# Two feed-forward layers' first 1024 inner columns taken token tile by token tile, with ScalarE-only evacuations and casts, later conditioning and packed planner priorities

## The chip, the cores and the metric

One NeuronCore of a Trainium2 chip runs the whole program. The metric is device time in microseconds of one execution. The core has five engines that run side by side: TensorE (PE; its weight loads are listed as PEld), VectorE (DVE), ScalarE (ACT), GpSimd (POOL) and SyncE (SP, here only the queue that issues weight loads).

## The reference, cut to what matters

Two blocks of two layers each work on 256 tokens by 1024 features, in float32. Layer i of the first block is

```python
mod = silu(c) @ ada_w[i] + ada_b[i]               # c: one vector of 1024
sh1, sc1, g1, sh2, sc2, g2 = split(mod, 6)        # "conditioning": six vectors of 1024
h = rms_norm(x, norm_mix[i]) * (1 + sc1) + sh1
x = x + g1 * mixer(h)                             # i=0 chunked attention, i=1 gated MLP (gmlp)
h = rms_norm(x, norm_ffn[i]) * (1 + sc2) + sh2
x = x + g2 * (square(relu(h @ ffn_w1[i])) @ ffn_w2[i])   # 1024 -> 4096 -> 1024
```

The second block runs two attention layers (`block2`), each a normalisation, eight projections, two kinds of attention, an output projection and a normalisation of its result.

## The kernel before, in words

**Tiles.** The 256 tokens are two tiles of 128, t=0 and t=1. All weights come from HBM as one stream of items of 128 by 1024 floats (`ITEMS`), two items to a DMA, into a ring of four such pairs. For a product close to float32 precision an item is split: `item` casts it to a rounded high half (L881 on ACT, L882 on DVE), and DVE subtracts that from the original for the low half (L885). A product then is three matmuls, L782 to L784 (`mm3`). Split items lie in one arena `R` with the transposed activations `hT` and the hidden activations: at most `NHL = 9` of them, and one is placed only if `SPARE = 5120` of the arena's 25 x 1024 + 256 floats per partition stay free beside it. Each takes 2048.

**Feed-forward (`ffn`).** `norm_T` transposes the normalised rows of a token tile (L810), applies the conditioning (L1015, L1021: shift number 3, scale number 4) and splits the result (L988, L990). Inner columns come in blocks of 128. Most blocks are made by `ws_block`: eight 256-wide products with the weight as the stationary side, both token tiles at once. The first 512 columns are made by rows (`xs_group`): for one token tile at a time, eight 512-wide products, an evacuation (`copy`), four transposes, then relu and square (`relu2`). The second matrix follows `LAGF` blocks behind, accumulating in four banks, and `out_proj` finishes token tile 0 ahead of tile 1 for the last `tail` blocks. `gate_finish` multiplies by the gate, adds to x (L721), and normalises (`norm_scale`: L931 or L933, L731, L695, L968 or L970).

**Conditioning.** A 1024 by 1024 piece of `ada_w` is eight items. They come as columns (`adc`: one DVE reduction per item, L748, result ready for one block of 128 features) or as rows (`adg`, for the pairs in `BY_ROWS`: DVE accumulates over the eight items, L740, then `fin_gate` sums over partitions with PE products L770 and evacuates).

**Order.** Nothing is issued in program order. Every operation is recorded with its engines, an estimated duration and the buffers it touches; `Sched.round` places operations one by one, and the order that results is written into each engine's queue. Operations with two entries in `alts` are placed on either engine. `schedule` makes four rounds; from each it works out when an operation is due (PE's at its start, the rest counted back from their users) and uses that as the next round's priority; the best round is kept. At run time each engine works through its queue in order and waits on semaphores.

## Time and profile before

| what | value |
|---|---|
| median of three runs (lowest, highest) | 1009.37 us (1007.86, 1009.71) |
| the profiled execution's own time | 1009.61 us |
| its span, first to last instruction | 1007.8 us |
| PE busy, DVE busy, ACT busy | 97%, 77%, 56% of the span |
| mean granted TensorE clock | 0.992 |
| weights and inputs read from HBM | 214.48 MB |
| mean rate of all DMAs | 215 GB/s |

The stages lie in the trace like this, in us from the span's start: the first projections to about 62, attention to about 117, its output projection to about 147, feed-forward 0 to about 345, gmlp to about 558, feed-forward 1 to about 735, the two attention layers of the second block to 1002, and the last normalisation. Matmuls are pipelined, so that a row of a busy PE shows more than the time to the next matmul; the spacing of starts tells the cost of one. A stage's own waits tell more than the shares of the whole span.

### The profile page before, as it was taken

The numbers are of one execution on the slowest core, as the hardware profiler recorded it, in microseconds if no ns is written. First come the engines' busy times: TensorE is split into PE (matmuls) and PEld (weight loads), VectorE is DVE, ScalarE is ACT, GpSimd is POOL, SyncE is SP. The second block draws the span as 40 slices with busy tenths as digits, with TensorE's granted clock in tenths as the row PEclk, the third lists the DMA queues.
The fourth block names the chain that finished last, engine by engine and source line by source line (L and its number), as shares of the span: only waits on it lengthen the run. The fifth ranks groups of instructions, "written<-read, shape, count | busy, mean of one in ns | idle before, by whom it ended". The sixth has DMA issues, their size and how long they took to land.

```text
span 1007.8 us, 14849 instructions
## 1 busy us (share of the span) xinstructions
PE 976.2 (97%) x5716; PEld 851.7 (85%) x5716; DVE 776.7 (77%) x1308; ACT 568.0 (56%) x1052; POOL 24.7 (2%) x60
## 2 busy tenths in 40 slices
PE   6999988999999999999999999999999999899997
PEld 5768776899999888899999899999989888799886
DVE  6899989988877986977767855645697786877982
ACT  6578736544445655644455744445455676655781
POOL 1000000010000000000000000030000000000000
PEclk9999998999999999999999999999999999899999
DMA  8987585898775595766463555565545333443401
GB/s 321 359 316 263 210 334 183 359 364 324 290 281 203 207 383 204 292 228 232 170 242 133 177 197 172 207 193 203 179 161 188 113 121 119 160 168 128 166 1 42
DMA packets 32121, 216.50 MB, mean 215 GB/s; under 512 B 3825, under 2 KB 4081, under 8 KB 7217
## 3 DMA queue, kind: packets, MB, share of 16 engines
q1 hardware_dynamic: 30816, 211.98, 56.9%
q0 software_dynamic: 1232, 3.56, 1.4%
q8 instruction: 45, 0.74, 0.3%
q14 instruction: 28, 0.22, 0.1%
HBM read 214.48 MB, written 1.05 MB: 214 GB/s over the span
## 4 chain that ended last, share of the span: by engine, by line
PE 79%; DVE 9%; ACT 5%; DMA 4%; issue 2%; SPq 0%; DVEq 0%; ACTq 0%
PE banks L782 24%; PE banks L783 24%; PE banks L784 24%; PE banks L770 4%; DMA raw<-in_wall 4%; DVE arena_r L885 3%; PE banks L810 3%; DVE arena L721 2%; ACT arena_r L881 1%; ACT arena L695 1%; DVE arena L740 1%; DVE arena L748 1%; DVE arena_r L990 1%; DMA arena<-in_xin 1%; ACT arena L710 1%
## 5 line engine op out<-in xcount | busy, mean ns | idle before, releaser
L782 PE MATMUL banks<-arena_r 128*128 128x256 f32 (+1 forms) x1632 | 563.9, 346 | 7.7 <-ACT arena_r L988 5.2
L783 PE MATMUL banks<-arena_r 128*128 128x256 f32 (+1 forms) x1632 | 554.0, 339 | 1.5 <-DVE arena_r L885 1.4
L784 PE MATMUL banks<-arena_r 128*128 128x256 f32 (+1 forms) x1632 | 553.4, 339 | 1.6 <-DVE arena_r L990 1.6
L885 DVE TENSOR_TENSOR arena_r<-raw,arena_r 128x1024 fp32r<-128x1024 f32 x300 | 359.7, 1221 | 41.8 <-ACT arena_r L881 40.4
L782 PEld LDWEIGHTS banks<-arena_r 128*128 128x128 f32 x1632 | 310.9, 191 | 43.3 <-ACT arena_r L988 8.9
L784 PEld LDWEIGHTS banks<-arena_r 128*128 128x128 f32 x1632 | 310.5, 190 | 38.3 <-DVE arena_r L990 4.7
L783 PEld LDWEIGHTS banks<-arena_r 128*128 128x128 f32 x1632 | 311.2, 191 | 35.3 <-DVE arena_r L885 4.6
L881 ACT CAST arena_r<-raw 128x1024 fp32r<-128x1024 f32 x265 | 270.5, 1044 | 85.9 <-DMA raw<-in_wall 43.4
L695 ACT ACTIVATE arena<-banks 128x256 f32<-128x256 f32 (+1 forms) x104 | 45.0, 434 | 147.2 <-PE banks L784 145.1
L988 ACT ACTIVATE arena_r<-arena 128x256 fp32r<-128x256 f32 (+1 forms) x120 | 55.8, 475 | 78.5 <-DVE arena L740 49.6
L740 DVE SCALAR_TENSOR_TENSOR arena<-banks,arena 128x256 f32<-128x256 f32 (+1 forms) x84 | 38.1, 453 | 60.7 <-ACT arena L695 42.8
L748 DVE CUSTOM_DVE_ANT_0 arena<-raw,arena 128x1024 f32<-128x1024 f32 x56 | 71.7, 1281 | 14.5 <-DMA raw<-in_wall 13.1
L695 ACT ACTIVATE arena<-arena 128x256 f32<-128x256 f32 (+8 forms) x159 | 65.1, 416 | 23.9 <-DVE arena L740 9.1
L990 DVE SCALAR_TENSOR_TENSOR arena_r<-arena,arena_r 128x256 fp32r<-128x256 f32 (+1 forms) x120 | 58.3, 494 | 24.6 <-ACT arena_r L988 23.1
L770 PE MATMUL banks<-arena 128*128 128x64 f32 (+4 forms) x448 | 70.3, 292 | 4.5 <-DMA arena<-in_ident 3.6
L770 PEld LDWEIGHTS banks<-arena 128*128 128x128 f32 x448 | 60.6, 196 | 10.1 <-ACT arena L695 3.6
L810 PE MATMUL banks<-arena 128*128 128x128 f32 x356 | 55.7, 281 | 10.1 <-DVE arena L731 4.3
L710 ACT COPY arena<-banks 128x512 f32<-128x512 f32 (+4 forms) x100 | 47.7, 488 | 31.2 <-PE banks L784 13.7
L810 PEld LDWEIGHTS banks<-arena 128*128 128x128 f32 x356 | 44.0, 147 | 21.5 <-DVE arena L731 4.6
L721 DVE TENSOR_TENSOR arena<-arena 128x512 f32<-128x512 f32 (+6 forms) x128 | 51.4, 433 | 7.6 <-ACT arena L695 3.2
L740 DVE SCALAR_TENSOR_TENSOR arena<-raw,arena 128x1024 f32<-128x1024 f32 x40 | 51.3, 1282 | 3.8 <-DMA raw<-in_wall 3.6
L721 DVE TENSOR_TENSOR arena<-banks,arena 128x512 f32<-128x512 f32 (+1 forms) x48 | 30.0, 641 | 15.3 <-PE banks L784 6.8
(45 smaller groups left out, 330.5 us busy)
## 6 DMA issues: line engine op xcount, KB each, us to landing
raw<-in_wall SPq DMA_DIRECT2D x194, 1024.0 KB, 4.9
raw<-in_wall SPq DMA_DIRECT2D x8, 512.0 KB, 9.1
arena<-in_nbias SPq DMA_DIRECT2D x4, 512.0 KB, 6.5
arena<-in_rows POOLq DMA_DIRECT2D x3, 512.0 KB, 6.0
arena<-in_xin SPq DMA_DIRECT2D x2, 512.0 KB, 5.9
out_dram<-arena SPq DMA_DIRECT2D x4, 256.0 KB, 2.4
arena<-in_dbias POOLq DMA_DIRECT2D x2, 384.0 KB, 3.6
arena<-in_wsT POOLq DMA_DIRECT2D x1, 512.0 KB, 5.9
```

Source lines behind the costliest of these rows:

```text
L695: nc.scalar.activation(out=res(out), in_=res(in_), func=func, scale=res(scale), **kw, **({"accum_out": res(accum)} if accum is not None el ...
L721: alt = ("DVE", 0.068 + n / 960.0, lambda: nc.vector.tensor_tensor(out=res(out), in0=res(a), in1=res(b), op=op))
L740: return self.S.op(("DVE", dur, lambda: nc.vector.scalar_tensor_tensor(out=res(out), in0=res(a), scalar=res(s), in1=res(b), op0=op0, op1=o ...
L748: return self.S.op(("DVE", dur, lambda: nc.vector.tensor_tensor_reduce(out=res(junk if out is None else out), in0=res(a), in1=res(b), scal ...
L770: o = self.S.op(("PE", max(n, 96) * 0.00167, lambda: nc.tensor.matmul(res(out), lhsT=res(l), rhs=res(r), start=start, stop=stop)), rd, [ou ...
L782: nc.tensor.matmul(o, lhsT=lh, rhs=rh, start=start, stop=False)
L783: nc.tensor.matmul(o, lhsT=lh, rhs=rl, start=False, stop=False)
L784: nc.tensor.matmul(o, lhsT=ll, rhs=rh, start=False, stop=stop)
L810: nc.tensor.transpose(res(o), res(i), res(ident))
L881: alts = [("ACT", 0.093 + D / 1200.0, lambda: nc.scalar.copy(out=res(hi), in_=res(src))), ("DVE", 0.068 + D / 1920.0, lambda: nc.vector.te ...
L885: dve = ("DVE", 0.068 + D / 960.0, lambda: nc.vector.tensor_tensor(out=res(lo), in0=res(src), in1=res(hi.f32()), op=ALU.subtract))
L990: self.S.op(("DVE", 0.068 + n / 960.0, lambda: nc.vector.scalar_tensor_tensor(out=res(lo), in0=res(src), scalar=scale, in1=res(hi.f32()), ...
```

## The change

The first 1024 columns of each feed-forward's inner width, not the first 512, are made by rows (`XG = 2`): tile 0's two groups, then tile 1's. The second matrix now follows eight blocks behind the first. High halves of weights are cast by ACT alone, and six kinds of evacuations and scalings of the attention that DVE could take stay on ACT. The shift of feed-forward 0 (layer 0, number 3) is now taken by columns. The conditioning of layer 1 moves back in the stream: gate 2 from the first feed-forward into gmlp's first part, gate 5 from gmlp into feed-forward 1. The second token tile's input is loaded with the first one's, ahead of all weights. The planner's due times are counted with PE's gaps taken out, and the best round's priorities are placed once more to give the order.

```diff
-BY_ROWS = ((0, 2), (0, 5), (1, 2), (1, 5), (0, 3))
+BY_ROWS = ((0, 2), (0, 5), (1, 2), (1, 5))
-LAGF = 5
+LAGF = 8
+XG = 2
-    s += pair_stream(NFF, ("w1", 0), ("w2", 0), LAGF, ada_items(0, (5,)) + ada_items(1, (0, 1, 2)))
-    e = ada_items(1, (3, 4, 5))
+    s += pair_stream(NFF, ("w1", 0), ("w2", 0), LAGF, ada_items(0, (5,)) + ada_items(1, (0, 1)))
+    e = ada_items(1, (2, 3, 4))
-    s += pair_stream(NFF, ("w1", 1), ("w2", 1), LAGF)
+    s += pair_stream(NFF, ("w1", 1), ("w2", 1), LAGF, ada_items(1, (5,)))
...
             if best is None or self.clock < best[0]:
-                best = self.clock, [(o, alt, tab, [b.off for b in o.bufs]) for o, alt, tab in out], \
-                    {b: b.off for b in self.fixed}, [(o, o.eng, o.start, o.fin) for o in self.ops]
-            due = {}
+                best = self.clock, [o.pri for o in self.ops]
+
+            due, packed, gaps, last = {}, {}, 0.0, 0.0
+            for o in sorted((o for o in self.ops if o.eng == "PE"), key=lambda o: o.start):
+                gaps += max(o.start - last, 0.0)
+                packed[o], last = o.start - gaps, o.fin
             for o in sorted(self.ops, key=lambda o: o.start, reverse=True):
-                t = o.start if o.eng == "PE" else self.clock
+                t = packed[o] if o.eng == "PE" else last - gaps
...
-            self.prev_split = S.op(alts[:1] if i < POS["w1", 0, 0] else alts, [src], [hi], after=after, pri=pri,
+            self.prev_split = S.op(alts[:1], [src], [hi], after=after, pri=pri,
...
-        self.hooks[1] = [lambda pri: load(self.x[1].v(), io["xin"][:, 1, :], 1.46, pri)]
+        load(self.x[1].v(), io["xin"][:, 1, :], 1.46, -2000)
...
-            self.act(nb[i].v(), nb[i].v(), D, scale=-1.0, dve=True)
+            self.act(nb[i].v(), nb[i].v(), D, scale=-1.0)
-                self.act(qT.v(), ps.v()[:, 0:256], 256, scale=gqk.v(), psum=True, dve=True)
+                self.act(qT.v(), ps.v()[:, 0:256], 256, scale=gqk.v(), psum=True)
...
                 for t in range(2):
-                    row = self.F(512)
-                    self.copy(row.v(), self.xs_group(t, hT, [("w1", l, q) for q in range(4)], 512, 2, (4, 5)).v(), 512,
-                              psum=True)
...
+                    for g in range(XG):
+                        row = self.F(512)
+                        self.copy(row.v(), self.xs_group(t, hT, [("w1", l, 4 * g + q) for q in range(4)], 512, 2, (4, 5)).v(),
+                                  512, psum=True)
...
-            elif f >= 4:
+            elif f >= 4 * XG:
```

The attention's copies get `both=False` in the same way; the items of the first eight `w1` blocks are cut as rows of 512 columns. Lines after the planner's part move down by 18 or 19 (L885 becomes L903).

How the order moves is shown at one boundary, the end of attention's output projection and the start of feed-forward 0. First DVE's queue of the kernel before, from where token tile 0's rows are gated and added to x (L721), squared and summed (L933), scaled by the norm (L968), a low half (L885), the conditioning of the transposed rows (L1015):

```order
L721 TENSOR_TENSOR arena<-banks,arena 128x512 x2
L721 TENSOR_TENSOR arena<-arena 128x512 x2
L933 ISA arena<-arena 128x512
L933 ISA arena 128x1
L731 TENSOR_SCALAR arena<-arena 128x1
L721 TENSOR_TENSOR arena<-banks,arena 128x512 x2
L968 TENSOR_SCALAR arena<-arena 128x512
L885 TENSOR_TENSOR arena_r<-raw,arena_r 128x1024
L1015 TENSOR_SCALAR arena<-banks,arena 128x128 x4
L882 CAST arena_r<-raw 128x1024
```

The same place in the changed kernel, from the second half of tile 0's rows on:

```order
L739 TENSOR_TENSOR arena<-banks,arena 128x512
L739 TENSOR_TENSOR arena<-arena 128x512
L951 ISA arena<-arena 128x512
L951 ISA arena 128x1
L749 TENSOR_SCALAR arena<-arena 128x1
L903 TENSOR_TENSOR arena_r<-raw,arena_r 128x1024
L986 TENSOR_SCALAR arena<-arena 128x512
L903 TENSOR_TENSOR arena_r<-raw,arena_r 128x1024
L1033 TENSOR_SCALAR arena<-banks,arena 128x128 x4
L1008 SCALAR_TENSOR_TENSOR arena_r<-arena,arena_r 128x4x128 x2
```

Before, both halves of tile 0 come together and the gating of tile 1 (the second L721 row that reads banks) stands inside tile 0's chain; now the halves come one after the other, tile 1's gating stands behind tile 0's low halves (L1008), and the cast of DVE is gone.

PE's queue at the same place, before, from the last product of the output projection: the products of `fin_gate` for the shift, tile 0's transposes, the first product of feed-forward 0.

```order
L784 MATMUL banks<-arena_r 128x512
L770 MATMUL banks<-arena 128x1 x8
L810 MATMUL banks<-arena 128x128 x8
L782 MATMUL banks<-arena_r 128x512
L783 MATMUL banks<-arena_r 128x512
L784 MATMUL banks<-arena_r 128x512
```

And in the changed kernel, around tile 0's transposes:

```order
L802 MATMUL banks<-arena_r 128x512
L828 MATMUL banks<-arena 128x128 x8
L800 MATMUL banks<-arena_r 128x512
L801 MATMUL banks<-arena_r 128x512
L802 MATMUL banks<-arena_r 128x512
```

The eight one-column products are gone. In the whole queue, the products of both tiles' output projection alternated before and ended together, and four products lay between tile 0's and tile 1's transposes; now tile 0's last product is followed by twelve of tile 1 (six ahead of tile 0's transposes, six behind), and twelve products (36 rows) lie between the two tiles' transposes.

## Rows read from the trace of the kernel before

**Rows 1.** The page's first part: busy us of each engine (share of the span), instructions.
```profile
PE 976.2 (97%) x5716; PEld 851.7 (85%) x5716; DVE 776.7 (77%) x1308; ACT 568.0 (56%) x1052; POOL 24.7 (2%) x60
```

**Rows 2.** Busy time by stretch: length, then PE, PEld, DVE, ACT, POOL, PE clock, DMA share, GB/s.
```profile
62.00:117.00 55.00, 53.15 (x289) 41.66 (x287) 53.52 (x141) 46.59 (x126) 2.07 (x4) 1.00 0.65 234
117.00:145.50 28.50, 27.14 (x138) 21.51 (x138) 25.50 (x37) 12.49 (x23) 1.44 (x2) 1.00 0.82 310
145.50:153.40 7.90, 4.94 (x34) 4.27 (x32) 7.70 (x16) 5.00 (x14) 0.00 (x0) 0.92 0.58 233
153.40:170.90 17.50, 15.40 (x61) 11.52 (x62) 16.91 (x22) 11.78 (x25) 0.00 (x0) 0.84 0.45 150
...
190.00:411.00 221.00, 221.00 (x1276) 195.04 (x1275) 183.37 (x268) 117.07 (x186) 3.54 (x6) 1.00 0.74 279
...
573.00:734.00 161.00, 161.00 (x1027) 146.69 (x1027) 94.54 (x132) 73.20 (x112) 10.28 (x28) 1.00 0.57 194
...
749.00:868.00 119.00, 118.79 (x723) 104.81 (x723) 91.40 (x198) 77.74 (x166) 2.65 (x5) 1.00 0.43 150
868.00:879.00 11.00, 7.66 (x27) 5.69 (x26) 10.81 (x18) 8.94 (x21) 0.00 (x0) 0.70 0.19 68
```

**Rows 3.** Waits of PE over the span: in total, times, longest, in us.
```profile
PE banks L810 <- DVE arena L968: 1.6, 1, 1.6
...
PE banks L782 <- ACT arena L695: 1.3, 1, 1.3
PE banks L810 <- ACT arena L710: 1.3, 2, 0.9
```

**Rows 4.** Timeline of PE at the start of feed-forward 0: start, length, what, idle before.
```profile
150.63 1.09 PE L810 MATMUL banks<-arena 128*128 128x128 f32 x8 [1.28 <-ACT arena L970]
153.55 0.79 PE L782 MATMUL banks<-arena_r 128*128 128x512 f32 x1 [1.82 <-ACT arena_r L988]
...
157.33 0.80 PE L783 MATMUL banks<-arena_r 128*128 128x512 f32 x1 [0.43 <-DVE arena_r L885]
...
158.77 0.51 PE L783 MATMUL banks<-arena_r 128*128 128x512 f32 x1
```

**Rows 5.** Timeline of DVE in the same place.
```profile
145.67 1.37 DVE L721 TENSOR_TENSOR arena<-banks,arena 128x512 f32<-128x512 f32 x2 [0.38 <-PE banks L784]
...
150.16 0.48 DVE L968 TENSOR_SCALAR arena<-arena 128x512 f32<-128x512 f32 x1
```

**Rows 6.** Groups of DVE in 62 to 146 us: count, busy us, mean ns, idle before.
```profile
L748 DVE DVE_READ_ACCUMULATOR2_ANT arena<- 128x1 f32 x40 | 3.3, 83 | 0.0
...
L713 DVE COPY arena<-banks 128x512 f32<-128x512 f32 x2 | 1.4, 690 | 0.0
...
L701 DVE TENSOR_SCALAR arena<-banks,arena 128x256 f32<-128x256 f32 x3 | 1.3, 476 | 0.0
```

**Rows 7.** Groups over the span, shapes kept apart: the three kinds of weight splitting.
```profile
L885 DVE TENSOR_TENSOR arena_r<-raw,arena_r 128x1024 fp32r<-128x1024 f32 x300 | 359.7, 1221 | 41.8 <-ACT arena_r L881 40.4
...
L881 ACT CAST arena_r<-raw 128x1024 fp32r<-128x1024 f32 x265 | 270.5, 1044 | 85.9 <-DMA raw<-in_wall 43.4 <-PE banks L784 32.3 <-PE banks L783 6.4
...
L882 DVE CAST arena_r<-raw 128x1024 fp32r<-128x1024 f32 x35 | 23.9, 686 | 2.3 <-PE banks L784 2.1 <-DMA raw<-in_wall 0.2
```

**Rows 8.** Timeline of PE, 512-wide matmuls near the end: first and last of ten.
```profile
998.73 0.39 PE L784 MATMUL banks<-arena_r 128*128 128x512 f32 x1
...
1000.77 0.39 PE L784 MATMUL banks<-arena_r 128*128 128x512 f32 x1
```

**Rows 9.** Timeline of PE, 256-wide matmuls in gmlp: first and last of eighteen.
```profile
416.72 0.28 PE L782 MATMUL banks<-arena_r 128*128 128x256 f32 x1
...
418.76 0.28 PE L784 MATMUL banks<-arena_r 128*128 128x256 f32 x1
```

**Rows 10.** The chain that ended last, merged: one batch of eight transposes, and the input's load.
```profile
3.07 7.11 DMA arena<-in_xin
...
338.21 0.88 PE banks L810 x8
```

More of the change, by code (lines that the diff above doesn't have):

```diff
@@ L116, in item_array @@
         return a["a_w_out"][0][it[1] * P:(it[1] + 1) * P]
-    if n == "w1" and it[2] < 4:
-        w = a["ffn_w1"][it[1]][it[2] * 256:(it[2] + 1) * 256, 0:512]
+    if n == "w1" and it[2] < 4 * XG:
+        g, q = divmod(it[2], 4)
+        w = a["ffn_w1"][it[1]][q * 256:(q + 1) * 256, g * 512:(g + 1) * 512]
         return w.reshape(2, P, 512).transpose(1, 0, 2).reshape(P, D)
@@ L338 @@
     EXTRA = {"DVE": 0.6}
+    SHIFTS = ()
     def __init__(self):
@@ L423, in schedule, with shift @@
                 o.pri = due[o] - (self.RUSH if o.crit else 0.0)
-        self.clock = best[0]
-        for o, o.eng, o.start, o.fin in best[3]:
-            pass
-        for b in self.fixed:
-            b.off = best[2][b]
-        return best[1]
+        pri = list(best[1])
+        for seed in self.SHIFTS:
+            self.shift(best[1], pri, seed)
+        for o, o.pri in zip(self.ops, pri):
+            pass
+        out = self.round(spaces, slots)
+        return [(o, alt, tab, [b.off for b in o.bufs]) for o, alt, tab in out]
+    @staticmethod
+    def shift(base, pri, seed):
+        rng = np.random.default_rng(seed)
+        lo, hi = min(base), max(base)
+        mid, width = rng.uniform(lo, hi), rng.choice([8.0, 20.0, 60.0])
+        size, share = rng.choice([0.7, 2.0, 5.0]), rng.choice([0.1, 0.4, 1.0])
+        for i, b in enumerate(base):
+            if abs(b - mid) < width and rng.random() < share:
+                pri[i] += size * rng.standard_normal()
     def round(self, spaces, slots):
@@ L1191, in attention @@
             for t in range(2):
-                self.copy(qkv[j][n][t].v(), acc[t, j + 3 * n].v(), 512, psum=True)
+                self.copy(qkv[j][n][t].v(), acc[t, j + 3 * n].v(), 512, psum=True, both=False)
         def second(j):
@@ L1201, in second @@
             for t in range(2):
-                self.copy(qkv[j][1][t].v(), ps[t].v(), 512, psum=True)
+                self.copy(qkv[j][1][t].v(), ps[t].v(), 512, psum=True, both=False)
         def norms(n):
@@ L1241, in attention @@
                     self.copy(kk.v(i)[i * 64:(i + 1) * 64, i * 256:(i + 1) * 256], ps.v()[i * 64:(i + 1) * 64, 256:512], 256,
-                              psum=True)
+                              psum=True, both=False)
                 s1, s0 = self.bank(SB), self.bank(SB)
@@ L1258, in attention @@
             pT = self.F(384)
-            self.copy(pT.v(), ps.v()[:, 0:384], 384, psum=True)
+            self.copy(pT.v(), ps.v()[:, 0:384], 384, psum=True, both=False)
             g = h // 4
@@ L1294, in ffn @@
             self.norm_T(t, self.xss[t], hT, A, B)
-        gate = self.mod(l, 5) if l == 1 else None
         hid = {}
@@ L1308, in first @@
                 for t in range(2):
-                    row = self.F(512)
-                    self.copy(row.v(), self.xs_group(t, hT, [("w1", l, q) for q in range(4)], 512, 2, (4, 5)).v(), 512,
-                              psum=True)
-                    ps = self.bank((6, 7))
-                    self.tr([ps.v()[:, j * P:(j + 1) * P] for j in range(4)], [row.v()[:, j * P:(j + 1) * P] for j in range(4)])
-                    pair = relu2(ps, 512)
-                    for j in range(4):
-                        hid[j, t] = pair, j * P
-            elif f >= 4:
+                    for g in range(XG):
+                        row = self.F(512)
+                        self.copy(row.v(), self.xs_group(t, hT, [("w1", l, 4 * g + q) for q in range(4)], 512, 2, (4, 5)).v(),
+                                  512, psum=True)
+                        ps = self.bank((6, 7))
+                        self.tr([ps.v()[:, j * P:(j + 1) * P] for j in range(4)],
+                                [row.v()[:, j * P:(j + 1) * P] for j in range(4)])
+                        pair = relu2(ps, 512)
+                        for j in range(4):
+                            hid[4 * g + j, t] = pair, j * P
+            elif f >= 4 * XG:
                 pair = relu2(self.ws_block(hT, ("w1", l, f)), 256)
```

## The prediction

> **What bounds the kernel now.** I read the page's shares first: PE is busy 97% of the span, DVE 77%, ACT 56% [rows 1]. A share is a mean over stages, so I next read busy time by stretch [rows 2]. In the long middles nothing can be won but work of PE: 221.00 of 221.00 us in feed-forward 0 and gmlp's first part, 161.00 of 161.00 us in feed-forward 1. What PE loses lies at boundaries. The largest is the start of feed-forward 0: from 145.5 to 170.9 us PE stands still for 2.96 + 2.10 us, and the granted clock is 0.92 and 0.84 there. The second is the start of the last layer, 868 to 879 us: 3.34 us idle and a clock of 0.70. The waits of PE name three more places, of 1 to 2 us each [rows 3]. In attention, 62 to 117 us, PE is idle for 1.85 us, but DVE is busy for 53.5 of 55 us and ACT for 46.6: there all three are near full.
>
> Then I read the timeline at the largest boundary. PE waits 1.28 us for tile 0's scaled rows, transposes them, and waits 1.82 us for their high halves [rows 4]. Both waits come from a chain that starts when the projection's products have ended: the gating of tile 0 starts at 145.67 us and its rows are scaled at 150.16 us [rows 5]; the first product follows at 153.55 us. That is 7.9 us in which PE has little to do, since both tiles end together. After the idle time the clock is at its lower level, 1.2 GHz of the two: from 153.55 to 158.77 us PE starts 11 matmuls [rows 4], which at the later spacing of 2.04 us for nine [rows 8], 0.227 us each, take 2.5 us. The difference is 2.7 us, of which 0.43 us is a wait.
>
> **The change, part by part.** My sum is made against the profiled execution's own 1009.61 us; it lies 0.24 us above the median of the runs, which is within their spread.
>
> *The boundary to feed-forward 0.* What is lost there now is 2.96 + 2.10 us of idle time and 2.7 - 0.43 = 2.3 us of slow clock, 7.4 us together. In the new order tile 0's last product of the projection is followed by twelve of tile 1, each three matmuls of 0.227 us, 8.2 us in all. The chain from gating to first product was 153.55 - 145.67 = 7.9 us, and it is shorter now, because tile 1's gating no longer stands inside it. So it is covered. Tile 1's own chain has to be covered by tile 0's two groups, 16 products or 10.9 us, where one group of 5.4 us stood before. What is late next is the splitting of weights: tile 0's groups use an item every two products, 1.36 us, and a low half takes 1.22 us of DVE [rows 7]. Counting DVE's queue from tile 0's gating to the eighth `w1` item, at 0.65 us for a 512-wide operation [rows 5] and 1.2 us for a low half or anything else of 1024 columns [rows 7], I get some 21 us, against some 24 us until PE needs that item. It fits by about 3 us. I take 1.5 us as still lost, so -5.9 us; the bounds are all 7.4 us and only 2 us.
>
> *Evacuations that stay on ACT.* By the order, DVE loses in attention three scalings of 0.48 us, two copies of 0.69 us [rows 6] and two scalings of 1024 columns at about 0.7 us (as a cast of that size) [rows 7], 4.2 us; the shift by columns costs it eight reads of an accumulator, 0.7 us [rows 6]. DVE is the fuller engine there, so this 3.5 us could bring the end of attention forward; but ACT gets it with interest, and PE was idle for only 1.85 + 1.36 us between 62 and 145.5 us [rows 2]. Bounds: -3.2 us, and +1.5 us if ACT, at 46.6 of 55 us, holds up the softmax. I take -1.5 us, nearer to what PE's idle time allows.
>
> *Casts that stay on ACT.* 35 casts go from DVE to ACT [rows 7], that is, from 0.69 to 1.04 us. All belong to stages where PE is full and ACT is at 117 of 221 or 73 of 161 us [rows 2]; I cost them at nothing. If that cover were gone, each would cost the difference, 0.36 us, 12.5 us in all. Here a rule stands against the change. The Trainium skill, page Perfetto Trace Analysis, section Optimizing Scalar/DVE Operations, says that the engine with a DVE performance mode is the faster one, and that ScalarE should take work when DVE is saturated; the two rows agree on the speed, and in feed-forward 1 DVE, at 94.5 of 161 us, is not saturated. By that rule the sum would be up to 12.5 us higher; since PE had no gap in those 161 us, I keep nothing.
>
> *Row groups.* Per layer, four blocks by columns (96 matmuls of 256) become 48 matmuls of 512. At 2.04 us for seventeen [rows 9], 0.120 us each, that is 11.5 us removed and 10.9 us added; eight more transposes cost 0.88 us [rows 10]. Net +0.3 us on PE's full path, +0.6 us for two layers.
>
> *Waits at the other boundaries.* In gmlp PE waited 1.3 us for a bank that an activation, ACT L695, had to free [rows 3]; by the order that activation stood behind a switch of ACT's function table, the second pair of switches in a row. Now one pair is left there, and 27 products of 256 columns, not 8, run ahead of the first mixing product: -1.3 us. At feed-forward 1 PE waited 0.9 us for the copy of the row group [rows 3]; tile 1's transposes now have more products on both sides: -0.9 us. At the last layer eight instead of seven products cover tile 0's norm, one of 0.68 us out of the 1.6 us wait [rows 3]: -0.6 us, and the clock still falls.
>
> *Moves that cost nothing.* Conditioning of layer 1 moves by eight items from feed-forward 0 to later; DVE, at 183 of 221 us, and DMA, at 0.74, had room in the one and have more in the other. Gate 5 in feed-forward 1 adds eight accumulations, some 10 us at a low half's duration, to a stage with DVE at 59%. The early load of tile 1's input moves one 512 KB transfer ahead of the weights; the chain passes through that input [rows 10], but weights fill the queue behind it either way: 0, with 1.4 us on either side.
>
> Sum: -5.9 - 1.5 + 0.6 - 1.3 - 0.9 - 0.6 = -9.6 us, or **1000.0 us**.
>
> **The rivals.** *The wait moves to the weights* (A). The 3 us of room that I count in DVE's queue are used up by waits for raw items or free arena; PE then stops inside tile 0's groups and drops to the lower clock as it did after 153.55 us. For it: DVE is busy 16.9 of 17.5 us there now, and already makes PE wait for a low half at 157.33 us [rows 4]. Against it: DVE gives up 3.5 us before and two accumulations there. Price: 5 us of the 5.9 us, that is about 1005.
>
> *The order does not show on the chip* (B). The planner works with estimated durations, and its new priorities reorder the whole program; other places could lose what the boundary wins. Then the time is within 2 us of before. For it: nothing in the trace bounds a reorder of the second block. Against it: PE was idle there for only 0.21 of 119 us, so the old order had slack on the other engines, and the new one keeps the same work.
>
> *Fewer split weights fit* (C), the case that ends on the slower side. With eight blocks of lag instead of five, three more hidden blocks of 512 floats lie in arena `R`. Of its 25,856 floats the transposed activations take 4,096, six hidden blocks 3,072, now nine 4,608; with 5,120 spare, 6.6 and now 5.9 items of 2,048 fit: six, now five. Its place is every block of both feed-forwards; the price is a small wait of PE per block, 48 times. It decides from 0.25 us a block, 12 us, which makes 1012. For it: DVE is at 183 of 221 us in feed-forward 0. Against it: the same stretch shows no gap of PE with six, and in feed-forward 1 DVE has 41% free. The Trainium skill, page Perfetto Trace Analysis, section Optimization Strategy, says that a gap which repeats on the engine that should be full can mean that SBUF has no room for the next tile. By that rule, rows of before would show such gaps if the arena were already short; they show none.
>
> *The casts come onto the path* (D), 0.36 us each as above: 1012.5. Against it: ACT's free half.
>
> **How the numbers follow.** Forecast 60%, at 993 to 1004: 993 adds to the sum the whole boundary (1.5 us), the rest of PE's idle time before 145.5 us (1.7 us), the last layer's wait and slow clock (some 4 us); 1004 has the boundary at its lower bound. A has 20%, to 1007; B 11%; C 6% and D 3%. About 0.2%, 2 us, is what a measurement of this kernel can tell from no change. The range of **993 to 1007** holds the forecast and A, 80%. Faster by over 0.2%, below 1007.3 us: the forecast, A and a fifth of B, 82%. Within it: most of B, 8%. Slower: C, D and the rest of B, 10%.
>
> **What would show it.** Right: in the changed profile PE's waits between the transposes of tile 0 and the first product are gone, the clock stays at 1.0 from 140 to 170 us, gmlp's wait for an activation behind a table switch is gone, and the last layer still shows its drop. A: waits of PE for L903's low halves inside the first 32 row products, with a clock below 1. C: a PE busy time below the length of the stretch through both feed-forwards. D: waits of L801 or L800 for casts on ACT in feed-forward 1. I am wrong if the end of attention moves later by more than 2 us, since everything after it would have to make that up.

## The result, and the profile after the change

The changed kernel takes 996.36 us (median of four runs, 996.04 to 997.05) where the kernel before takes 1009.54 us in the same comparison. The ratio is 0.9866, with a 95% interval of 0.984 to 0.9892: about 13 us faster. The forecast was 1000.0 us and a gain of 9.6 us. The sum is right within its range, but several of its terms are not: attention came out worse than its bounds, the start of feed-forward 0 and the first 62 us came out better than theirs, and the last layer gained 3.8 us where 0.6 were forecast.

The first view is busy time by stretch, for the kernel before (new rows, in the stretches used below) and for the changed one. Columns: stretch and length, PE, PEld, DVE, ACT, POOL busy, PE clock, DMA share, GB/s. Before:

```profile
117.00:146.00 29.00, 27.64 (x140) 21.93 (x140) 25.84 (x38) 12.64 (x23) 1.44 (x2) 1.00 0.83 313
146.00:172.00 26.00, 20.95 (x102) 16.47 (x101) 25.38 (x37) 17.22 (x37) 0.00 (x0) 0.87 0.50 181
...
411.00:573.00 162.00, 159.72 (x1027) 144.57 (x1026) 121.65 (x178) 86.08 (x137) 0.00 (x0) 1.00 0.58 212
840.00:880.00 40.00, 36.66 (x173) 30.26 (x172) 31.66 (x53) 24.14 (x44) 0.00 (x0) 0.91 0.40 138
```

After, from several answers of the same view:

```profile
62.00:117.00 55.00, 49.23 (x251) 36.11 (x249) 52.09 (x137) 48.23 (x133) 0.93 (x3) 1.00 0.64 245
117.00:146.00 29.00, 26.96 (x143) 23.03 (x144) 26.08 (x51) 14.83 (x22) 1.45 (x2) 0.88 0.86 326
146.00:172.00 26.00, 26.00 (x128) 21.64 (x127) 24.74 (x31) 21.52 (x40) 0.00 (x0) 1.00 0.58 204
...
190.00:411.00 221.00, 221.00 (x1258) 194.44 (x1257) 167.76 (x230) 124.32 (x191) 3.04 (x5) 1.00 0.71 265
411.00:573.00 162.00, 162.00 (x1020) 146.14 (x1019) 121.74 (x192) 85.82 (x137) 1.45 (x2) 1.00 0.56 202
573.00:734.00 161.00, 161.00 (x987) 144.80 (x986) 103.72 (x140) 81.08 (x121) 10.29 (x28) 1.00 0.61 218
840.00:880.00 40.00, 38.56 (x195) 31.55 (x194) 31.96 (x56) 27.34 (x51) 0.00 (x0) 1.00 0.42 146
```

From 146 to 172 us PE is now never idle and the clock is 1.00, where 5.05 us were idle at a clock of 0.87. At 840 to 880 us the clock no longer falls. But from 62 to 146 us PE is idle for 5.77 + 2.04 us, where it was 1.85 [rows 2] + 1.36 us, and the slow clock is now here. The waits of PE (in total, times, longest) say the same:

```profile
PE banks L800 <- ACT arena L728: 4.8, 1, 4.8
...
PE banks L800 <- ACT arena_r L1006: 1.9, 2, 1.0
...
PE banks L801 <- DVE arena_r L903: 0.8, 2, 0.4
```

The waits for L968 and L695 [rows 3] are gone. New is one wait of 4.8 us near 114 us for an evacuation (L728, formerly L710). The start of feed-forward 0, which answers to [rows 4], now reads like this on PE: tile 0's transposes (147.52) stand between products of the projection's tile 1, tile 1's transposes follow at 156.61, and no row has a wait.

```profile
147.29 0.39 PE L802 MATMUL banks<-arena_r 128*128 128x512 f32 x1
147.52 1.04 PE L828 MATMUL banks<-arena 128*128 128x128 f32 x8
148.32 0.47 PE L800 MATMUL banks<-arena_r 128*128 128x512 f32 x1
...
156.61 1.04 PE L828 MATMUL banks<-arena 128*128 128x128 f32 x8
157.40 0.47 PE L800 MATMUL banks<-arena_r 128*128 128x512 f32 x1
```

To compare kernels in one number per stretch I use the time that PE **loses**: from the start of each matmul to the start of the next, less the spacing of that shape where nothing holds it (0.227 us for 512 columns of a split product, 0.120 us for 256 [rows 8, 9], 0.11 us for a transpose, and so on), summed over the matmuls that start in the stretch. It holds idle time and slow clock alike. What the matmuls need at these spacings fell from 937.0 to 935.7 us. The levels in the tables hang on the spacing taken for the small shapes (products of 64 columns start 0.06 us apart in some places and 0.11 us in others); the differences between kernels do not, and neither do the figures from 146 to 172 us.

| term of the sum | forecast | lost before, after (us) | measured |
|---|---|---|---|
| first 62 us (early load) | 0 | 14.5, 11.7 | -2.8 |
| attention, 62 to 146 us | -1.5 | 13.0, 20.3 | +7.3 |
| start of feed-forward 0, 146 to 172 us | -5.9 | 8.6, 0.2 | -8.4 |
| gmlp and feed-forward 1, 172 to 573 us | -2.2 | 10.3, 7.3 | -3.0 |
| start of the last layer, 840 to 880 us | -0.6 | 6.7, 2.9 | -3.8 |
| all other stretches | 0 | 7.6, 7.5 | -0.1 |
| matmuls themselves (row groups) | +0.6 | | -1.3 |
| first matmul starts earlier | 0 | | -0.4 |

The sum, -12.5 us, is the difference of the two spans, 1007.8 and 995.3 us.

### The profile page after: what moved, and what is told of

Same layout as the page of the kernel before. It is cut to its first block, busy times and chain, and to the rows that moved or that the text cites. A ratio compares the mean times of both kernels' runs of the same rounds, so it can differ in the third digit from the quotient of the medians.

```text
span 995.3 us, 14657 instructions
## 1 busy us (share of the span) xinstructions
PE 969.8 (97%) x5620; PEld 844.6 (85%) x5620; DVE 753.3 (76%) x1269; ACT 597.9 (60%) x1082; POOL 23.3 (2%) x58
## 4 chain that ended last, share of the span: by engine, by line
PE 84%; DVE 6%; ACT 4%; DMA 3%; issue 2%; SPq 0%; DVEq 0%; ACTq 0%
PE banks L800 26%; PE banks L801 26%; PE banks L802 26%; PE banks L788 4%; PE banks L828 3%; DMA raw<-in_wall 3%; DVE arena L766 2%; ACT arena_r L899 1%; DVE arena_r L903 1%; ACT arena L713 1%; DVE arena L739 1%; ACT arena L728 1%; DVE arena_r L1008 1%; ACT arena_r L1006 1%; DMA arena<-in_xin 1%
## 5 line engine op out<-in xcount | busy, mean ns | idle before, releaser
L800 PE MATMUL banks<-arena_r 128*128 128x512 f32 (+1 forms) x1600 | 557.6, 348 | 6.9 <-ACT arena L728 4.8
L801 PE MATMUL banks<-arena_r 128*128 128x512 f32 (+1 forms) x1600 | 546.6, 342 | 0.8 <-DVE arena_r L903 0.8
L802 PE MATMUL banks<-arena_r 128*128 128x512 f32 (+1 forms) x1600 | 546.3, 341 | 0.0
L903 DVE TENSOR_TENSOR arena_r<-raw,arena_r 128x1024 fp32r<-128x1024 f32 x300 | 360.4, 1221 | 71.1 <-ACT arena_r L899 70.1
L899 ACT CAST arena_r<-raw 128x1024 fp32r<-128x1024 f32 x300 | 305.2, 1043 | 60.3 <-PE banks L802 26.5
L800 PEld LDWEIGHTS banks<-arena_r 128*128 128x128 f32 x1600 | 303.8, 190 | 40.2 <-ACT arena L728 5.2
L802 PEld LDWEIGHTS banks<-arena_r 128*128 128x128 f32 x1600 | 303.4, 190 | 36.3 <-DVE arena_r L1008 1.4
L801 PEld LDWEIGHTS banks<-arena_r 128*128 128x128 f32 x1600 | 304.0, 190 | 33.9 <-DVE arena_r L903 3.1
L713 ACT ACTIVATE arena<-banks 128x256 f32<-128x256 f32 (+1 forms) x100 | 44.0, 444 | 143.7 <-PE banks L802 136.9
L1006 ACT ACTIVATE arena_r<-arena 128x256 fp32r<-128x256 f32 (+1 forms) x116 | 55.1, 484 | 64.7 <-DVE arena L758 38.2
L766 DVE CUSTOM_DVE_ANT_0 arena<-raw,arena 128x1024 f32<-128x1024 f32 x64 | 82.0, 1281 | 14.8 <-DMA raw<-in_wall 14.5
L713 ACT ACTIVATE arena<-arena 128x256 f32<-128x256 f32 (+9 forms) x161 | 67.3, 425 | 37.7 <-DVE arena L951 10.4
L1008 DVE SCALAR_TENSOR_TENSOR arena_r<-arena,arena_r 128x256 fp32r<-128x256 f32 (+1 forms) x116 | 57.8, 506 | 23.5 <-ACT arena_r L1006 22.7
L788 PE MATMUL banks<-arena 128*128 128x64 f32 (+3 forms) x432 | 67.6, 295 | 4.9 <-DMA arena<-in_ident 3.3
L728 ACT COPY arena<-banks 128x512 f32<-128x512 f32 (+3 forms) x105 | 50.1, 495 | 28.9 <-PE banks L828 13.0
L828 PE MATMUL banks<-arena 128*128 128x128 f32 x372 | 59.4, 287 | 6.9 <-ACT arena L988 4.5
L758 DVE SCALAR_TENSOR_TENSOR arena<-raw,arena 128x1024 f32<-128x1024 f32 x32 | 41.0, 1280 | 4.1 <-DMA raw<-in_wall 4.0
```

The lines of the kernel that those rows point to most:

```text
L713: nc.scalar.activation(out=res(out), in_=res(in_), func=func, scale=res(scale), **kw, **({"accum_out": res(accum)} if accum is not None el ...
L758: return self.S.op(("DVE", dur, lambda: nc.vector.scalar_tensor_tensor(out=res(out), in0=res(a), scalar=res(s), in1=res(b), op0=op0, op1=o ...
L766: return self.S.op(("DVE", dur, lambda: nc.vector.tensor_tensor_reduce(out=res(junk if out is None else out), in0=res(a), in1=res(b), scal ...
L788: o = self.S.op(("PE", max(n, 96) * 0.00167, lambda: nc.tensor.matmul(res(out), lhsT=res(l), rhs=res(r), start=start, stop=stop)), rd, [ou ...
L800: nc.tensor.matmul(o, lhsT=lh, rhs=rh, start=start, stop=False)
L801: nc.tensor.matmul(o, lhsT=lh, rhs=rl, start=False, stop=False)
```

## The experiments

Each kernel was timed in five rounds beside the kernel before, whose median in these comparisons was 1008.9 to 1011.2 us; differences of about 1 us between the kernels are not to be relied on. copies_dve, copies_act and casts_dve keep the changed kernel's order and alter only the entries named. All the others are ordered anew by the planner, since any edit changes the priorities; so each is read twice, by its time and by what its own trace shows at the place in question. This table is what the sections below read. "Left" is how many products of attention's output projection, all of tile 1, follow the last one of tile 0 in PE's order.

| kernel | median (us) | left | lost 0-62 | 62-146 | 146-172 | 172-573 | 840-880 | whole |
|---|---|---|---|---|---|---|---|---|
| before | 1009.5 | 2 | 14.5 | 13.0 | 8.6 | 10.3 | 6.7 | 60.8 |
| changed | 996.36 | 12 | 11.7 | 20.3 | 0.2 | 7.3 | 2.9 | 50.1 |
| copies_dve | 995.42 | 12 | 11.9 | 18.7 | 0.3 | 6.5 | 3.1 | 48.3 |
| copies_act | 996.13 | 12 | 12.7 | 19.5 | 0.2 | 6.9 | 2.9 | 49.9 |
| casts_dve | 997.83 | 12 | 12.7 | 18.6 | 0.4 | 7.4 | 3.0 | 50.8 |
| planner_only | 1008.15 | 3 | 14.8 | 17.3 | 7.8 | 10.2 | 4.4 | 61.8 |
| rows_alone | 1005.19 | 2 | 15.0 | 12.3 | 7.0 | 8.5 | 5.9 | 56.2 |
| att_undone | 1000.74 | 3 | 12.6 | 17.1 | 6.9 | 5.9 | 3.4 | 53.1 |
| rows_undone | 996.97 | 12 | 12.5 | 17.6 | 1.5 | 7.0 | 3.6 | 49.1 |
| gaps_kept | 993.09 | 12 | 13.1 | 14.3 | 2.2 | 6.1 | 2.9 | 46.1 |
| x1_late | 995.58 | 12 | 12.7 | 13.9 | 1.5 | 6.5 | 2.9 | 47.6 |
| order_shaken | 998.29 | 7 | 12.4 | 18.3 | 2.7 | 6.3 | 2.8 | 50.8 |
| cond_undone | 993.00 | 9 | 13.3 | 12.7 | 2.4 | 7.3 | 2.4 | 45.5 |
| shift_by_rows | 994.11 | 7 | 11.8 | 12.1 | 1.7 | 7.4 | 3.0 | 45.0 |

### The wait near 114 us: is ScalarE's queue the cause?

In the changed kernel PE waits at 114 us. On PE (idle before, and what ended it, in brackets):

```profile
113.83 0.40 PE L802 MATMUL banks<-arena_r 128*128 128x512 f32 x1
119.04 0.79 PE L800 MATMUL banks<-arena_r 128*128 128x512 f32 x1 [4.81 <-ACT arena L728]
...
125.44 0.48 PE L800 MATMUL banks<-arena_r 128*128 128x512 f32 x1
```

and on ACT at the same time, where the four evacuations (L728) stand behind exponentials (L713) and casts (L899):

```profile
113.81 1.03 ACT L899 CAST arena_r<-raw 128x1024 fp32r<-128x1024 f32 x1
114.75 0.51 ACT L713 ACTIVATE arena<-arena 128x256 f32<-128x256 f32 x1
...
117.33 1.04 ACT L899 CAST arena_r<-raw 128x1024 fp32r<-128x1024 f32 x1 [0.49 <-DMA raw<-in_wall]
118.40 1.84 ACT L728 COPY arena<-banks 128x512 f32<-128x512 f32 x4
```

It looks as if an engine's queue were the fault. Two kernels move just these four, to VectorE or to an earlier place on ScalarE; PE's queue stays word for word the same.

```diff
-                self.copy(qkv[j][1][t].v(), ps[t].v(), 512, psum=True, both=False)
+                self.copy_moved(j == 2, qkv[j][1][t].v(), ps[t].v(), 512)
...
-            self.copy(pT.v(), ps.v()[:, 0:384], 384, psum=True, both=False)
+            self.copy_moved(h in (8, 9), pT.v(), ps.v()[:, 0:384], 384)
...
-        out = self.round(spaces, slots)
+        out = self.pull(self.round(spaces, slots))
```

`copy_moved` marks the operation (and, in the first kernel, gives it to VectorE); `pull` moves it up in the finished order to just behind the products that it reads.

> The changed kernel with its own order of the work; only the four evacuations in ScalarE's queue that stand together where TensorE waits 4.8 us near 114 us (two of the last projection, two of transposed softmax rows) are made by VectorE, each just behind the products it evacuates. Theory 1 (evacuations that only ScalarE may make stand behind its exponentials and casts, and TensorE waits for them): the wait falls below 1.5 us, the clock stays at its upper level, and the time falls by 4 to 7 us, to 989 to 992.5. Theory 2 (the softmax as a whole is late, on VectorE as much as on ScalarE): another wait of TensorE of the same size takes its place within 10 us, and the time is 995 to 998.

> The same four evacuations stay on ScalarE and are only placed earlier in its queue, each just behind the products it evacuates. If ScalarE's order is the fault (theory 1a): as with VectorE, 989 to 992.5. If ScalarE is full there and lacks the 2 us (theory 1b): the wait moves to a later softmax row or weight, and the time is 994 to 997. Theory 2: 995 to 998.

Measured: 995.42 us (994.94 to 996.75) and 996.13 us (994.77 to 996.97), against 996.36. The one wait is gone, and with VectorE three others stand in its place, as PE's rows with a wait show:

```profile
115.47 0.50 PE L801 MATMUL banks<-arena_r 128*128 128x512 f32 x1 [1.68 <-DVE arena_r L903]
119.68 0.93 PE L828 MATMUL banks<-arena 128*128 128x128 f32 x6 [2.12 <-ACT arena L728]
129.59 0.79 PE L828 MATMUL banks<-arena 128*128 128x128 f32 x4 [2.16 <-DVE arena L739]
```

6.0 us instead of 4.8: a low half of a weight, softmax rows, and the normalised result of a group of heads. With the earlier place on ScalarE, PE waits 4.0 us for the evacuation of a later softmax row (L728). That fits theory 1b as well as theory 2: in copies_act no row of ScalarE shows a wait from 112 to 121 us. It is copies_dve that speaks for theory 2, with three waits in place of one of the same size: ScalarE is relieved there, and now stands idle for 1.07 us near 115 us until VectorE has made a step of the softmax (L766). So theory 1 falls. The end of attention as a whole is late in this order, VectorE is busy for 52.1 of the 55 us before it, and a wait that is removed there is followed by the next. Its two stretches show that PE's idle time even rises, from 7.8 to 8.8 us; the 1 us that this kernel gained fits the clock, which stays at 1.00:

```profile
62.00:117.00 55.00, 50.51 (x259) 37.66 (x259) 53.26 (x138) 48.26 (x131) 0.93 (x3) 1.00 0.68 248
117.00:146.00 29.00, 24.72 (x145) 20.76 (x143) 28.35 (x55) 14.59 (x24) 1.45 (x2) 1.00 0.83 327
```

### The casts

The 35 casts of [rows 7] go back to VectorE, each at its place in the changed kernel's order.

```diff
-            self.prev_split = S.op(alts[:1], [src], [hi], after=after, pri=pri,
-                                   kind=("hi", it))
+            self.prev_split = S.op(alts[:1], [src], [hi], after=after, pri=pri,
+                                   kind=("hi", it)); it in ON_DVE and S.move.append((self.prev_split, alts[1], False))
```

> The changed kernel with its own order of the work; only the 35 weight casts that VectorE made before are made by VectorE again, each at its place. The prediction's step (casts cost nothing, since TensorE is full in their stages): 994.5 to 998.5, no difference beyond 2 us. Rival (casts on VectorE lengthen the chains at boundaries: the start of feed-forward 0 and of the last layer): at least one of these two shows a wait of TensorE over 2 us or a stretch at the lower clock, and the time is 999 to 1004.

Measured: 997.83 us (996.99 to 999.5). The groups of casts in its trace read as in [rows 7]:

```profile
L899 ACT CAST arena_r<-raw 128x1024 fp32r<-128x1024 f32 x265 | 270.4, 1043 | 54.0 <-DMA raw<-in_wall 26.1 <-PE banks L802 21.6 <-PE banks L801 3.2
L900 DVE CAST arena_r<-raw 128x1024 fp32r<-128x1024 f32 x35 | 24.0, 686 | 0.4 <-PE banks L802 0.4
```

Neither boundary lost more than 0.2 us by it, and the second block about 1 us outside of its boundary; the rival falls, and the step stands within its 2 us. The difference of 1.5 us is hardly more than can be relied on; in the two traces 1.0 us more is lost in the first 62 us, where both kernels issue the same instructions. Each cast is 0.36 us shorter on VectorE, and the kernel is not faster for it. The Trainium skill, page Perfetto Trace Analysis, section Optimizing Scalar/DVE Operations, says that VectorE is the faster engine where it has a performance mode, and that moving work to ScalarE may make sense where VectorE is saturated. The rows agree on the speed, but the gain does not show here; in feed-forward 1, where VectorE is busy for 103.7 of 161 us after the change, only six of the 35 casts lie, so that 2.1 us at most could have shown.

### What closes the start of feed-forward 0?

Four kernels take the change apart: the planner rules alone, the row groups alone, and the change without its evacuations or without its row groups. Edits: the kernel before with the new `schedule`; the kernel before with `XG = 2`, `LAGF = 8` and their items; and, from the changed kernel,

```diff
-LAGF = 8
-XG = 2
+LAGF = 5
+XG = 1
```

or, for the evacuations,

```diff
-                self.copy(qkv[j][n][t].v(), acc[t, j + 3 * n].v(), 512, psum=True, both=False)
+                self.copy(qkv[j][n][t].v(), acc[t, j + 3 * n].v(), 512, psum=True)
...
-                self.act(qT.v(), ps.v()[:, 0:256], 256, scale=gqk.v(), psum=True)
+                self.act(qT.v(), ps.v()[:, 0:256], 256, scale=gqk.v(), psum=True, dve=True)
```

> The kernel before with the new planner rules alone (gaps taken out of due times, the best round's priorities placed once more). Theory P (the boundary to feed-forward 0 is closed by the new priorities): idle time and slow clock there, 7.4 us before, fall below 3 us, and the time is 1000 to 1004. Theory G (it takes the second row group of each tile to cover the other tile's chain): more than 5 us stay lost there and the time is 1005 to 1010.

> The kernel before with the row groups and the lag of eight blocks alone. Its order still alternates tiles in attention's output projection. Theory 3: tile 0's two waits and the slow clock after them stay (5 us or more lost between 145 and 172 us), tile 1's wait and the one at feed-forward 1 go: 1003 to 1007. Theory G: under 3 us lost, 1000 to 1003.

> The changed kernel with one row group per tile and a lag of five blocks, as before; all else as changed, ordered anew. In the order that comes out, twelve products of tile 1's projection still follow tile 0's last, six ahead of tile 0's transposes and six behind. Theory 3 (finishing tile 0 first covers the boundary, the second row group hardly matters there): under 2 us lost between 146 and 172 us, time 996 to 1000. Theory G (tile 1's chain needs two groups of cover): 3 us or more are lost there or just behind, time 1000 to 1004.

> The changed kernel without one part: VectorE may again make the six kinds of evacuations and scalings of attention; the planner orders all anew. In the order that comes out, the products of attention's output projection alternate between the two token tiles again, as before the change. Theory 3 (the loss near 114 us and the gain at the start of feed-forward 0 are two ends of one bargain: by which tile's projection is finished first): the 4.8 us wait near 114 us is gone, over 5 us are lost again between 145 and 172 us, and the time is 998 to 1004. Theory 1 (ScalarE-only evacuations just cost time): the wait is gone, the start of feed-forward 0 stays closed, 989 to 992.5.

Measured: 1008.15 us for the planner alone (ratio 0.9991, 0.9976 to 1.0007: no change), 1005.19 us for the row groups alone (0.9965, 0.9946 to 0.9985), 996.97 us without the row groups (0.9865, 0.9833 to 0.9897: as the changed kernel), and 1000.74 us without the evacuations (0.9905, 0.9877 to 0.9932). Without the evacuations the two waits of [rows 4] are back on PE:

```profile
151.95 1.42 PE L828 MATMUL banks<-arena 128*128 128x128 f32 x8 [2.22 <-ACT arena L988]
154.87 0.79 PE L800 MATMUL banks<-arena_r 128*128 128x512 f32 x1 [1.50 <-ACT arena_r L1006]
```

and the stretches 146 to 172 us are, without evacuations and then without row groups:

```profile
146.00:172.00 26.00, 22.28 (x97) 17.69 (x96) 24.36 (x38) 20.25 (x38) 0.00 (x0) 0.87 0.50 186
```

```profile
146.00:172.00 26.00, 25.75 (x143) 21.43 (x142) 24.97 (x32) 20.83 (x40) 0.00 (x0) 1.00 0.66 235
```

So theory G falls: with one group per tile 1.5 us are lost, with two groups but alternating tiles 7.0. Theory P falls too: the planner rules alone leave 7.8 us lost. planner_only does not tell theories G and 3 apart, since its order has only three products left. What sorts the orders is how many products of tile 1 are left when tile 0's last one is issued. In the eleven different orders of the table the four with 2 or 3 left lose 6.9 to 8.6 us, the seven with 7 to 12 left lose 0.2 to 2.7. The four are just those in which VectorE may make attention's evacuations; each order with ScalarE alone finishes tile 0 first. So the count and the choice of engine go together in all eleven orders. That it is the count is borne out by copies_dve, which gives four evacuations back to VectorE in the changed kernel's order (it makes seven evacuations and scalings in the kernel before, between 62 and 146 us) and loses 0.3 us at the boundary, and by the two waits of att_undone, which end on tile 0's own chain. Why the planner answers to that part in this way was not tested further.

The other half of theory 3, a bargain in which the boundary's gain is paid for near 114 us, did not hold: without the evacuations 17.1 us are still lost from 62 to 146 us, and the next kernels close the boundary at far less.

### Is the loss in attention a price, or the draw of an order?

Five kernels leave out or undo one small part each. Due times that keep the gaps:

```diff
-                gaps += max(o.start - last, 0.0)
+                gaps += 0.0 * max(o.start - last, 0.0)
```

the late load of tile 1's input, the shift by rows, and the earlier conditioning (this one with `LAGF = 9` and eight planning rounds):

```diff
-        load(self.x[1].v(), io["xin"][:, 1, :], 1.46, -2000)
+        self.hooks[1] = [lambda pri: load(self.x[1].v(), io["xin"][:, 1, :], 1.46, pri)]
...
-BY_ROWS = ((0, 2), (0, 5), (1, 2), (1, 5))
+BY_ROWS = ((0, 2), (0, 5), (1, 2), (1, 5), (0, 3))
...
-    e = ada_items(1, (2, 3, 4))
+    e = ada_items(1, (3, 4, 5))
```

and priorities shaken at random over the first 180 us with nothing else changed (`SHIFTS = (167,)`).

> The changed kernel with due times that keep TensorE's gaps, as before; the priorities of the best round are still placed once more. If taking the gaps out is what gave the new order: 999 to 1005. If it is not needed beside the other parts: 993 to 998, with tile 0's projection still finished first, and by the order only 12 products behind it.

> The changed kernel with tile 1's input loaded behind the first weights, as before; ordered anew, and the order still finishes tile 0's projection 12 products ahead. TensorE loses 14.5 us in the first 62 us in the kernel before, 11.7 to 13.1 in the kernels with the early load. Theory E (the early load gives that gain, and it lasts to the end): 14 to 15 us lost there, and 998 to 999.5. The prediction's step (the load costs and gives nothing): 995 to 997.5; a loss in the first 62 us alone is made up in attention, whose end waits for the softmax anyway.

> The changed kernel, all parts as they are; only the priorities of the operations of the first 180 us are shaken at random (2 us each way). By its order tile 0's projection is finished six products ahead of tile 0's transposes and one product stands behind them, not six. Theory 3 (what is lost is decided by this order, not by the parts): 3 to 6 us lost between 145 and 172 us, and the time is 998 to 1003. Rival (the parts decide, the order is within noise): 995.5 to 997.5.

> The changed kernel with the conditioning of layer 1 back at its earlier places in the stream, a lag of nine blocks, and eight planning rounds instead of four. By its order tile 0's projection is finished 12 products ahead of tile 1's, with ten before its transposes and two behind. If the later conditioning gave the gain of 1.6 us between 190 and 430 us: 3.5 us are lost there again and the time is 996 to 999. If not: about 2 us there, and 993 to 996.

> The changed kernel with feed-forward 0's shift (layer 0, number 3) by rows again, ordered anew: eight one-column products of TensorE stand between tile 0's last projection product and its transposes once more, and three products of tile 1 follow the transposes, not six. Theory 3 (the order of the two tiles decides the boundary): 2 to 4 us lost between 145 and 172 us, less where attention ends earlier, and a time of 995 to 999. The prediction's step (the shift by columns gives 0.7 us at most): 996 to 997.5. If the shift is what gave the gain in the first 62 us, TensorE loses 14 us or more there again, and 998 to 1001.

Measured: 993.09 us (992.42 to 995.79), 995.58 (994.79 to 998.76), 998.29 (997.14 to 1001.52), 993.00 (991.98 to 997.8) and 994.11 us (993.68 to 996.57). In the stretch 62 to 146 us they lose 14.3, 13.9, 18.3, 12.7 and 12.1 us, where the changed kernel loses 20.3 and the kernel before 13.0; from 146 to 172 us all of them lose 1.5 to 2.7. Of the two stretches of attention that is, with gaps kept:

```profile
62.00:117.00 55.00, 50.71 (x264) 38.11 (x263) 52.74 (x134) 49.40 (x135) 0.67 (x2) 1.00 0.68 256
117.00:146.00 29.00, 28.82 (x162) 24.27 (x162) 28.11 (x57) 18.75 (x35) 1.46 (x2) 1.00 0.84 311
```

So the loss in attention is no price of the boundary, or at most the 1 to 2 us by which these orders lose more there. It belongs to the changed kernel's own order, and four of the five, which undo quite unlike parts, are without most of it. With the gaps kept, the kernel lies at the fast end of the second case: it is not slower but 3.3 us faster than the changed one, so taking the gaps out is not what gave the new order. x1_late bears out that the early load gives nothing: 12.7 us lost in the first 62, as in the other kernels with it, and the time is within the expected 995 to 997.5. shift_by_rows shows that the shift by columns is not the source of the gain in the first 62 us either (11.8 lost). cond_undone came out mixed: 3.5 us are lost from 190 to 430 us, where 2.1 are in the changed kernel, as the first case said, but the time is at the lower end of what the second case gave, since it loses 7.6 us less in attention. That the conditioning's place is the reason is not shown either: PE is idle for 1.07 us from 190 to 430 us in cond_undone, and for just as long in shift_by_rows, whose conditioning stands where the changed kernel has it. order_shaken lands at the lower edge of theory 3's range, with 2.7 us lost at the boundary where I expected 3 to 6: 2 us are lost by moving priorities about, with every part in place. shift_by_rows came out 1 us below its range.

Three versions (gaps kept, conditioning earlier, shift by rows) have lower medians than both kernels, with ratios to the kernel before of 0.9832 (0.9799 to 0.9865), 0.9845 and 0.9845 (both 0.982 to 0.9871). These intervals overlap with the changed kernel's, so that a gain over it is not shown for the last two; all four runs with gaps kept lie below all four of the changed kernel.

## Why the prediction was right, and where it was not

The largest term was right in kind, since the boundary to feed-forward 0 is closed by the order that the prediction read. That the sum lies so near is in part luck: attention missed its term by 8.8 us one way, and all other terms together by 11.7 us the other.

**The boundary to feed-forward 0** (-5.9 us, measured -8.4). The mechanism was right: tile 0's last product followed by twelve of tile 1 covers the chain from gating to first product. The room in VectorE's queue that I counted held too, and the 1.5 us that I took as still lost were 0.2. That the second row group is needed to cover tile 1's chain was a wrong step: one group leaves 1.5 us. The measured term exceeds the upper bound of 7.4 us, since lost time as counted here also holds the slower starts just behind each wait, which busy time hides. The bound itself was 0.2 us too low: eleven starts are ten spacings, so that the slow clock behind 153.55 us cost 2.5 us, not 2.3.

**Evacuations that stay on ScalarE** (-1.5 us, bounds -3.2 to +1.5; the stretch measured +7.3). This is the step that failed. I bounded the gain by PE's idle time there and the loss by ScalarE's room, as if the order stayed and only durations moved. It did not stay: in the changed order a wait of 4.8 us and the slow clock behind it take 8.3 us between 113 and 125.5 us, and copies_dve and copies_act show that no single queue is at fault. The part's real effect is elsewhere: without it the projection's tiles alternate and the kernel is 4.4 us slower. My own test, that I am wrong if attention ends more than 2 us later, was met: by 146 us PE had done 110.8 us of matmuls at full spacing, before the change 114.8. The start of feed-forward 0 made it up.

**Casts** (0): within 2 us, as forecast, though not for the reason given. Not all 35 casts belonged to stages where PE is full: in the trace of before, four start between 144 and 181 us, at and around the boundary that the change closes, and one at 865.67 us, within tile 0's chain at the last layer. casts_dve shows that casts there cost these boundaries 0.2 us at most.

**Row groups** (+0.6 us, counted -1.3): the eight one-column products of the shift, 16 rows of 0.11 us, were taken out and I had not counted them; in rows_alone, which keeps them, the matmuls need 0.5 us more than before, as the forecast had it. The groups' other effect is about the 0.9 us at feed-forward 1: the wait there is gone in rows_alone and falls to 0.3 us in rows_undone, which still loses about 1 us more from 411 to 573 us than the changed kernel.

**Waits at gmlp and feed-forward 1** (-2.2 us, -3.0): both went, as their rows said.

**The last layer** (-0.6 us, -3.8). I forecast that the clock still falls; it does not. PE's rows there, where the chain from tile 0's last evacuation to its first product used to leave a wait of 1.6 us [rows 3] and one of 1.7 us, are now

```profile
859.64 0.39 PE L802 MATMUL banks<-arena_r 128*128 128x512 f32 x1
859.99 1.09 PE L828 MATMUL banks<-arena 128*128 128x128 f32 x8
862.11 0.50 PE L800 MATMUL banks<-arena_r 128*128 128x512 f32 x1 [1.03 <-ACT arena_r L1006]
```

Counting products was not enough: the chain itself became shorter. From ScalarE's first read of the finished projection to the transposes it was 863.60 to 870.60 us, 7.0 us; it is 853.95 to 859.99, 6.0 us. ScalarE's row before and after:

```profile
863.60 0.60 ACT L931 ACTIVATE arena<-banks 128x512 f32<-128x512 f32 x1 [1.67 <-PE banks L784]
```

```profile
853.95 0.60 ACT L949 ACTIVATE arena<-banks 128x512 f32<-128x512 f32 x1
```

The casts are not the reason, since casts_dve keeps the gain. planner_only has 2.3 of the 3.8 us; the rest was not taken apart.

**The first 62 us** (0, -2.8). All kernels built from the changed one lose 11.7 to 13.3 us there, the three others 14.5 to 15.0. Neither the early load nor the shift, the evacuations, the row groups, the due times nor the conditioning is it alone. PE's own order there is the same in all fourteen kernels. PE waits for halves of the activations 2.7 us in the kernel before (L988 and L990) and 0.9 us in the changed one (L1006), but 2.8 us in cond_undone, which also loses less than before. What it is stays open.

**The rivals.** A (waits on weights at feed-forward 0) did not come: no low half makes PE wait there. C (too few split weights) did not: PE is busy for 221.00 of 221.00 and 161.00 of 161.00 us. D did not. B, that the new order does not show on the chip, did not come for the change as a whole; planner_only alone is such a case.

## What to carry to other kernels

Where a scheduler orders the whole program, price a change by the order that it brings out, not by the durations that it moves: here one part's worth (4.4 us) lay 30 us downstream of where it acted, and nearly the same work in other orders spread over 5 us. At a boundary between stages, count what one tile still has to do when the other tile's last product is issued; that number sorted all the orders tried here. And a wait that a trace shows as one engine's queue is worth an experiment that moves just that entry before it is called the cause.

## What the runs showed of the hardware

In these traces one long wait cost more than several short ones of about the same sum. After the 4.81 us wait at 114 us PE ran at the lower clock until 125.44 us, with matmuls of 512 columns 0.43 us apart and not 0.227, and the granted clock from 113 to 125.5 us was 0.73:

```profile
113.00:125.50 12.50, 7.69 (x30) 5.53 (x28) 11.07 (x28) 9.56 (x25) 0.00 (x0) 0.73 0.66 241
```

In copies_dve three waits of 1.68, 2.12 and 2.16 us, 4 and 10 us apart, left it at 1.00 throughout, while two waits of 2.22 and 1.50 us with only eight transposes between them, in att_undone, brought it to 0.87 for the stretch. These are single cases, and no rule is drawn from them. In the first 62 us the clock differs between executions of the very same instructions: 1.00 in the changed kernel and copies_dve (11.7 and 11.9 us lost), 0.92 in copies_act and casts_dve (12.7 each). A difference of 1 us there is no effect of a change.
